# HGRN2's dots, level scores, values and states as 64 x 64 products in the quarters of TensorE

## Chip, core and metric

The kernel runs on one core of one Trainium2 chip. The metric is the device time of one execution in microseconds (us); of several runs the median is given. TensorE (PE) multiplies matrices, VectorE (DVE) and ScalarE (ACT) work element by element, GpSimd (POOL) and SyncE (SP) mostly start transfers here. SBUF is the working memory with 128 partitions; PSUM holds TensorE's results in eight banks of 128 x 512 float32.

## What is computed

A decoder trunk of two layers on 512 tokens of width 1024. Each layer is: half a SwiGLU feed-forward, a mixer with one input projection and one output projection over three groups of heads (short convolution, HGRN2, forgetting attention "FoX"), and again half a SwiGLU. Everything is float32. HGRN2 has 4 heads with 64 key and 64 value features and runs over 8 chunks of 64 tokens:

```python
bcum = jnp.cumsum(lfb, axis=-2)
rel = bcum[..., :, None, :] - bcum[..., None, :, :]
decay = jnp.where(causal, jnp.exp(jnp.where(causal, rel, 0.0)), 0.0)
scores = jnp.einsum('bhtd,bhsd,bhtsd->bhts', qb, kb, decay)
o = (jnp.einsum('bhts,bhsv->bhtv', scores, vb)
     + jnp.einsum('bhtd,bhdv->bhtv', qb * jnp.exp(bcum), state))
b_last = bcum[..., -1:, :]
state = (jnp.exp(b_last[..., 0, :])[..., None] * state
         + jnp.einsum('bhsd,bhsv->bhdv', kb * jnp.exp(b_last - bcum), vb))
```

After that o is normalised per head, scaled and gated.

## The kernel before

**The whole.** The feed-forwards take most of the time. Their weights and activations are split into a high and a low part for TensorE (`parted`, `granule`, the tiles `hl`), so each product is three matmuls (`mm3`, lines 308, 314, 315). The mixer's projections go the same way: `stream_steps` loads a granule of two k-tiles of weights by a transfer on SP's queue, ACT copies its high part (line 297), DVE subtracts to get the low part (line 298), and TensorE runs 24 matmuls on it. There are three buffers for split granules.

**HGRN2's stage** is the generator `hgrn` (line 1183), once for each pair of heads (`pr` 0 and 1), so four times in a run. The two heads of a pair lie in partitions 0 to 63 and 64 to 127 (features), and 512 tokens in the columns. `mix` (lines 1079 to 1087) steps the two generators by turns, and after each step it lets one granule of the FoX projections run (`dense`). That sets the program's order on every engine: a small burst of HGRN2's matmuls, then 24 matmuls of a projection, then the burst of the other pair. A scheduler may shift single instructions; each engine then runs its own queue in order.

The steps of one pair are:
- the decays, `b`, `k`, `kb` (to line 1209), and the transposed keys (line 1222);
- the chunks' own states U, 16 products of 64 rows by 64 columns (line 1244), each in one quarter of TensorE: its rows are chosen by the chunk's parity, its columns by the head, and the two row halves write to two PSUM banks. A scan on DVE joins them to the states S (line 1254), laid out as S[partition, v, chunk], with the chunk innermost;
- seven levels. The scores inside a chunk are split by the highest bit in which two tokens differ, so level `lev` joins the later half of each block of 2w tokens with its earlier half, w = 2^lev / 2. Levels 0 and 1 need only a dot product per token (`e` times `heads2`, line 1276; heads2 is a 128 x 2 matrix that sums each head's 64 features). Levels 2 to 6 make `e` (two DVE operations, lines 1302 and 1303, and an exponential on ACT), then `e2`, the later halves times the queries (line 1308), and multiply 128 tokens at a time, all 128 features held, against both heads' queries (line 1317). The two heads are kept apart by `q2`: a copy of q for each head in which the other head's 64 rows are zero (lines 1049 to 1055, with POOL's memsets and SP's copies). The scores of both chunks of a 128-token tile and of both heads come out, cross-chunk ones included; a predicated copy with a mask (line 1320) puts the wanted ones into A, a tile of [128, 2 heads, 4, 128];
- S2 (lines 1289 to 1295): the states copied by ACT into 128 x 128 blocks, one per chunk, zero off the two heads' diagonal blocks;
- the values (line 1331: 8 products, 128 x 64 held) and the states (line 1338: 7 products, S2's blocks held, 64 columns of `qe` moving) are summed in one PSUM bank of the tag "po";
- Square and a copy by ACT (lines 1344 and 1345), the mean by a matmul with `ones_blk` (line 1348), normalisation, gate and the split for the output projection (to line 1357).

PSUM banks go by tags: "mm" three, "sc" two, "pt" two, "po" one. All levels of both pairs take one "sc" bank each; U and the transposes take "pt"; the FoX projections take "mm" and once "po". The FoX projections' results are taken out of their banks by `fox_qkv` (lines 1395 to 1413), on ACT and DVE.

Of the kernel before, what the change touches and what calls it, by code (L numbers as in the profile page):

```python
# [8 lines left out]
F32 = mybir.dt.float32  # L9
F32R = mybir.dt.float32r  # L10
BF16 = mybir.dt.bfloat16
U8 = mybir.dt.uint8
# [11 lines left out]
P = 128  # L24
T = 512
# [19 lines left out]
CH = 64  # L45
# [111 lines left out]
class Trunk:  # L157
# [32 lines left out]
    def build_consts(self, scratch):  # L190
# [10 lines left out]
        self.heads2 = c.tile([P, 2], F32, tag="heads2", name="heads2")  # L201
        nc.vector.memset(self.heads2, 0.0)
        for h in range(2):
            nc.vector.memset(self.heads2[64 * h : 64 * h + 64, h : h + 1], 1.0)
# [8 lines left out]
        self.lmask = c.tile([P, 6, P], U8, tag="lmask", name="lmask")  # L213
# [16 lines left out]
        for l in range(1, 7):  # L230
            nc.vector.tensor_scalar(a, xf, scalar1=float(2 ** (l - 1)), scalar2=None, op0=ALU.is_ge)
            nc.vector.tensor_scalar(b, xf, scalar1=float(2**l), scalar2=None, op0=ALU.is_lt)
            nc.vector.tensor_mul(a, a, b)
            nc.vector.tensor_mul(self.lmask[:, l - 1, :], a, later)
# [733 lines left out]
    def mix(self, l, w, w_out, conv_w, out_gain, q_gain, k_gain, f_bias, next_gain):  # L968
# [3 lines left out]
        with tc.tile_pool(name=self.n("mix"), bufs=1) as mp:  # L972
# [47 lines left out]
            with tc.tile_pool(name=self.n("hg"), bufs=1) as hp:  # L1020
# [28 lines left out]
                q2 = [mp.tile([P, 2, T], F32, tag=f"hy{i}", name=self.n("q2")) for i in range(2)]  # L1049
                for i in range(2):  # L1050
                    nc.vector.tensor_mul(q[i], bq[i], inv)
                    for hh in range(2):
                        r = slice(64 * hh, 64 * hh + 64)
                        nc.gpsimd.memset(q2[i][r, 1 - hh, :], 0.0)
                        nc.sync.dma_start(q2[i][r, hh, :], q[i][r, :])
# [16 lines left out]
                run = [self.hgrn(l, pr, hp, z[pr], q[pr], q2[pr], v, sg[pr], og) for pr in range(2)]  # L1072
# [110 lines left out]
    def hgrn(self, l, pr, hp, z, q, q2, v, sg, og):  # L1183
# [76 lines left out]
        A = own("A", [P, 2, 4, P])  # L1260
        A8 = A.rearrange("p h i t -> p (h i) t")
        for lev in range(7):
# [3 lines left out]
            if lev < 2:  # L1266
# [7 lines left out]
                sb = self.bank("sc")  # L1274
                for i in range(4):
                    nc.tensor.matmul(
                        sb[:, i:8:4], e[:, i * P : (i + 1) * P], self.heads2, start=True, stop=True
                    )
                d = sb[:, :8].unsqueeze(2)
                if lev == 0:  # L1280
                    nc.vector.tensor_mul(
                        A8, self.ident.unsqueeze(1).to_broadcast([P, 8, P]), d.to_broadcast([P, 8, P])
                    )
                else:
                    m = self.lmask[:, 0, 1::2].unsqueeze(1).to_broadcast([P, 8, P // 2])
                    nc.vector.copy_predicated(A8[:, :, 1::2], m, d.to_broadcast([P, 8, P // 2]))


                    S2 = own("lk", [P, NCH - 1, P])
                    for hh in range(2):  # L1290
                        o = slice(64 * hh, 64 * hh + 64)
                        nc.gpsimd.memset(S2[o, :, 64 - 64 * hh : P - 64 * hh], 0.0)
                        nc.scalar.copy(
                            S2[o, :, o], S[o, :, : NCH - 1].rearrange("p v c -> p c v")
                        )
                yield
# [8 lines left out]


            e2 = tmp().rearrange("p (h t) -> p h t", h=2)
            nc.vector.tensor_mul(
                e2.rearrange("p h (n w) -> p h n w", w=w),
                half(e, 1).unsqueeze(1).to_broadcast([P, 2, n2, w]),  # L1310
                q2.rearrange("p h (n two w) -> p h n two w", two=2, w=w)[:, :, :, 1, :],
            )
            sb = self.bank("sc")
            s2 = sb.rearrange("p (h t) -> p h t", h=2)
            for i in range(4):
                t = slice(64 * i, 64 * i + 64)
# [303 lines left out]
```

## Time and profile before

| what | value |
|---|---|
| median of 3 runs | 1860.53 us (1856.95 to 1863.77) |
| the profiled execution | 1854.12 us |
| its span, first to last instruction | 1852.3 us |
| TensorE's granted clock | 1.000 |
| busy: POOL | 177.3 us (10%) |
| HGRN2's burst matmuls, PE busy over both layers | dots 7.6, levels 21.5, values 4.4, states 7.1 us |
| U's matmuls, PE busy over both layers | 2.8 us for 128 records |

A profile is of one execution. Its rows name the source line (L1317), the engine, the operation, output and input tiles with buffer numbers left out (`sc<-t,t`), the shape, how many, and how long. PE stands for matmuls and PEld for the loads of held operands; a float32 matmul shows as two records of each. Matmuls are pipelined and the end of each is modelled, so the times at which they start say more than their lengths. What ended an idle time is inferred from semaphores.

### The profile page before, as it was taken

To read this page: it belongs to the slowest core of one execution; us is meant where nothing else is said; L and a number is where in the kernel's file an instruction comes from. 1 tells how busy PE (TensorE), PEld (TensorE's weight loads), DVE (VectorE), ACT (ScalarE), POOL (GpSimd) and SP (SyncE) were. 2 spreads that over 40 slices of the span, in tenths; PEclk is the share of its full clock that TensorE was granted. 3 is DMA by queue.
4 is the path that set the end of the run, shared out by engine and by line. 5 is a ranking of instruction groups with operands and counts; after the bars stand their busy time and mean duration, and the time that the engine had idled before them with its cause. 6 is when DMAs were issued, how large, how long until landed. Compare 5 with 4: busy or idle time off the path is not lost.

```text
span 1852.3 us, 33371 instructions
## 1 busy us (share of the span) xinstructions
PE 1829.1 (99%) x13536; PEld 1700.0 (92%) x13536; DVE 1480.2 (80%) x2101; ACT 1007.3 (54%) x1467; POOL 177.3 (10%) x182
## 2 busy tenths in 40 slices
PE   8999999999999999999999999999999999999999
PEld 6899999899877899999889999998998788999997
DVE  7889787678787888878678887966868878888883
ACT  5455555564665555555445555545546664555552
POOL 0011120100000001112001111201000000020210
PEclk9999999999999999999999999999999999999999
DMA  7658783232223767868265787813323228577762
GB/s 205 171 121 190 182 176 96 69 95 73 75 75 97 209 131 170 186 170 171 81 200 127 163 192 185 171 59 90 81 64 87 80 91 228 148 160 194 150 136 91
DMA packets 245417, 251.90 MB, mean 136 GB/s; under 512 B 19568, under 2 KB 230000, under 8 KB 245264
## 3 DMA queue, kind: packets, MB, share of 16 engines
q1 hardware_dynamic: 191664, 183.69, 32.5%
q0 software_dynamic: 53600, 66.09, 22.3%
q8 instruction: 106, 1.74, 0.4%
q14 instruction: 47, 0.39, 0.1%
HBM read 223.98 MB, written 2.10 MB: 122 GB/s over the span
## 4 chain that ended last, share of the span: by engine, by line
PE 88%; DVE 6%; ACT 3%; issue 2%; DMA 1%; SPq 0%; ACTq 0%; DVEq 0%
PE mm L308 13%; PE mm L315 13%; PE mm L314 13%; PE sc L308 6%; PE sc L315 6%; PE sc L314 6%; PE pt L308 6%; PE pt L314 6%; PE pt L315 6%; PE po L308 3%; PE po L314 3%; PE po L315 3%; PE po L1472 1%; DVE hl L298 1%; PE pt L1513 1%
## 5 line engine op out<-in xcount | busy, mean ns | idle before, releaser
L766 ACT CAST hl<-w 128x1024 fp32r<-128x1024 f32 x322 | 337.2, 1049 | 317.2 <-PE mm L315 76.5
L768 DVE TENSOR_TENSOR hl<-w,hl 128x1024 fp32r<-128x1024 f32 x322 | 392.8, 1222 | 90.8 <-ACT hl L766 90.7
L298 DVE TENSOR_TENSOR hl<-st,hl 128x512 fp32r<-128x512 f32 (+2 forms) x196 | 166.5, 852 | 114.7 <-ACT hl L297 113.6
L297 ACT CAST hl<-st 128x512 fp32r<-128x512 f32 (+2 forms) x196 | 146.6, 750 | 184.8 <-PE mm L315 66.7
L308 PE MATMUL mm<-xc,hl 128*128 128x256 f32 (+1 forms) x732 | 201.7, 276 | 1.7 <-ACT g L872 1.4
L315 PE MATMUL mm<-xc,hl 128*128 128x256 f32 x728 | 201.4, 277 | 0.0
L314 PE MATMUL mm<-xc,hl 128*128 128x256 f32 x728 | 201.4, 277 | 0.0
L308 PE MATMUL sc<-xc,hl 128*128 128x256 f32 (+1 forms) x530 | 146.6, 277 | 2.4 <-ACT g L872 1.7
L315 PE MATMUL sc<-xc,hl 128*128 128x256 f32 x528 | 146.3, 277 | 0.0
L314 PE MATMUL sc<-xc,hl 128*128 128x256 f32 x528 | 146.2, 277 | 0.0
L308 PEld LDWEIGHTS mm<-xc,hl 128*128 128x128 f32 x732 | 137.4, 188 | 2.5 <-ACT g L872 1.8
L315 PEld LDWEIGHTS mm<-xc,hl 128*128 128x128 f32 x728 | 136.7, 188 | 0.1
L314 PEld LDWEIGHTS mm<-xc,hl 128*128 128x128 f32 x728 | 136.7, 188 | 0.0
L308 PE MATMUL pt<-xc,hl 128*128 128x256 f32 (+1 forms) x484 | 133.0, 276 | 0.0
L314 PE MATMUL pt<-xc,hl 128*128 128x256 f32 x480 | 133.0, 277 | 0.0
L315 PE MATMUL pt<-xc,hl 128*128 128x256 f32 x480 | 132.8, 277 | 0.0
L308 PE MATMUL mm<-hl,x 128*128 128x256 f32 (+1 forms) x384 | 112.3, 292 | 0.7 <-DVE qk L1403 0.3
L308 PE MATMUL mm<-x,hl 128*128 128x512 f32 x272 | 109.7, 403 | 0.0
L315 PE MATMUL mm<-hl,x 128*128 128x256 f32 (+1 forms) x384 | 107.4, 280 | 0.0
L314 PE MATMUL mm<-hl,x 128*128 128x256 f32 (+1 forms) x384 | 107.1, 279 | 0.0
L315 PE MATMUL mm<-x,hl 128*128 128x512 f32 x272 | 106.5, 392 | 0.0
L314 PE MATMUL mm<-x,hl 128*128 128x512 f32 x272 | 106.0, 390 | 0.0
(478 smaller groups left out, 5678.2 us busy)
## 6 DMA issues: line engine op xcount, KB each, us to landing
w<-in_ffn_w_in_dram SPq DMA_DIRECT2D x140, 512.0 KB, 5.5
w<-in_ffn_w_out_dram SPq DMA_DIRECT2D x64, 512.0 KB, 4.2
w<-in_ffn_w_out_dram POOLq DMA_DIRECT2D x56, 512.0 KB, 8.6
st<-in_w_mix_in_dram SPq DMA_DIRECT2D x88, 256.0 KB, 2.7
st<-in_ffn_w_in_dram SPq DMA_DIRECT2D x72, 256.0 KB, 3.1
w<-in_ffn_w_in_dram POOLq DMA_DIRECT2D x35, 512.0 KB, 8.5
w<-S POOLq DMA_DIRECT2D x35, 512.0 KB, 4.7
st<-in_ffn_w_out_dram SPq DMA_DIRECT2D x24, 512.0 KB, 3.6
```

Source lines behind the costliest of these rows:

```text
L297: a = nc.scalar.copy(hi, src[:, c : c + w])
L298: b = nc.vector.tensor_sub(lo, src[:, c : c + w], hi)
L308: i = nc.tensor.matmul(acc[:, c], ah, bh[:, c], start=first and c.start == 0, stop=False, skip_group_check=True,)
L314: nc.tensor.matmul(acc, ah, bl, start=False, stop=False, skip_group_check=True)
L315: i = nc.tensor.matmul(acc, al, bh, start=False, stop=last, skip_group_check=True)
L766: A(nc.scalar.copy(hi, src))
L768: return lambda: V(nc.vector.tensor_sub(lo, src, hi))
L1472: nc.tensor.matmul(self.ob[:, t0 + u * P : t0 + 2 * P], V[:, j, h % 4].rearrange("p a d -> p (a d)"), part[:, j, u:, :].rearrange("p i t - ...
L1513: nc.tensor.transpose(tb[:, j * P : (j + 1) * P], p[:, j * P : (j + 1) * P], self.ident)
```

## The change

It does the following, for each pair of heads:
- `q2` goes, with its memsets on POOL and its copies on SP; `e2` is `e`'s later half times q, 256 columns instead of 512.
- A new inner function `scores` makes each level from 16 products: 64 features of one head held for one chunk, against that head's and chunk's queries (32 columns), or against a column of ones (1 column) for the dots. The row half is the head, the column half the chunk's parity, and the two heads write to two banks.
- A is [128, 2, 4, 64]: the parity of the chunk lies in the partition halves, so masks are 64 wide (`lmask`, `ident2`) and a level's predicated copy is two, one per head, of a quarter of the elements each.
- Pair 0 takes both "sc" banks and pair 1 both "pt" banks for a level and for the output; the mean takes "po".
- S2 goes, with its memsets and ACT's copies: S itself is the held operand of the states, 14 products of 64 x 64 in the two quarters on the diagonal.
- The states come before the values, with a step between them, and the values are 16 products in all quarters. The output lies in two banks: ACT copies from them, DVE adds the part that the other bank holds, and Square reads the sum from SBUF.

Changed line numbers: the changed file is five lines longer at its end. The core of the diff (constants left out):

```diff
-    def hgrn(self, l, pr, hp, z, q, q2, v, sg, og):
+    def hgrn(self, l, pr, hp, z, q, v, sg, og):
...
-        A = own("A", [P, 2, 4, P])
-        A8 = A.rearrange("p h i t -> p (h i) t")
+        A = own("A", [P, 2, 4, CH])
+        rows = [slice(CH * x, CH * x + CH) for x in range(2)]
+        tag = ("sc", "pt")[pr]
+
+        def scores(held, moving, n):
+            sb = [self.bank(tag) for _ in range(2)]
+            for i in range(4):
+                for hh, par in ((0, 0), (1, 1), (0, 1), (1, 0)):
+                    c = 2 * i + par
+                    nc.tensor.matmul(
+                        sb[hh][rows[par], i * n : (i + 1) * n],
+                        held[rows[hh], c * CH : (c + 1) * CH], moving(rows[hh], c),
+                        start=True, stop=True,
+                    )
+            return [x[:, : 4 * n] for x in sb]
...
-                    S2 = own("lk", [P, NCH - 1, P])
-                    for hh in range(2):
-                        o = slice(64 * hh, 64 * hh + 64)
-                        nc.gpsimd.memset(S2[o, :, 64 - 64 * hh : P - 64 * hh], 0.0)
-                        nc.scalar.copy(
-                            S2[o, :, o], S[o, :, : NCH - 1].rearrange("p v c -> p c v")
+                for hh, d in enumerate(scores(e, lambda r, c: self.ones_c[r, :], 1)):
+                    n = CH >> lev
+                    d = d.unsqueeze(2).to_broadcast([P, 4, n])
+                    if lev == 0:
+                        nc.vector.tensor_mul(
+                            A[:, hh], self.ident2.unsqueeze(1).to_broadcast([P, 4, n]), d
                         )
+                    else:
+                        m = self.lmask[:, 0, 1::2].unsqueeze(1).to_broadcast([P, 4, n])
+                        nc.vector.copy_predicated(A[:, hh, :, 1::2], m, d)
...
+            e2 = tmp()[:, : T // 2]
             nc.vector.tensor_mul(
...
+                e2.rearrange("p (n w) -> p n w", w=w), half(e, 1), half(q, 1)
+            )
+            sb = scores(e, lambda r, c: e2[r, 32 * c : 32 * c + 32], 32)
+            for hh in range(2):
+                nc.vector.copy_predicated(
...
+        ob = [self.bank(tag) for _ in range(2)]
+        for c in range(1, NCH):
+            for hh in range(2):
                 nc.tensor.matmul(
...
+                    ob[hh][rows[hh], c * CH : (c + 1) * CH], S[rows[hh], :, c - 1],
+                    qe[rows[hh], c * CH : (c + 1) * CH],
+                    start=c == 1, stop=False, skip_group_check=True,
                 )
...
+        yield
         for i in range(4):
...
+            for par, hh in ((0, 0), (1, 1), (0, 1), (1, 0)):
+                c = 2 * i + par
                 nc.tensor.matmul(
...
+                    ob[par][rows[hh], c * CH : (c + 1) * CH],
+                    v[rows[par], i, pr * P + 64 * hh : pr * P + 64 * hh + 64],
+                    A[rows[par], hh, i, :], start=i == 0 and par != hh, stop=i == 3,
+                    skip_group_check=True,
                 )
...
-        nc.scalar.activation(sq, ob, AF.Square)
-        nc.scalar.copy(o, ob)
+        every = lambda a, c: a.rearrange("p (c t) -> p c t", t=CH)[:, c::2, :]
+        for hh in range(2):
+            f, mine, other = rows[hh], ob[hh], ob[1 - hh]
+            nc.scalar.copy(o[f, hh * CH :], mine[f, hh * CH :])
+            if hh:
+                nc.scalar.copy(o[f, :CH], other[f, :CH])
+            c = 1 + hh
+            nc.vector.tensor_add(every(o[f, :], c), every(o[f, :], c), every(other[f, :], c))
+        nc.scalar.activation(sq, o, AF.Square)
         yield
-        mb = self.bank("sc")
+        mb = self.bank("po")
```

71 lines of the change are left out of this document (19 added, 52 removed).

## The prediction

> **What bounds the kernel now.** I read the page first, then busy time by stage, then TensorE's (PE's) instructions in order of time.
>
> ```profile
> PE 1829.1 (99%) x13536; PEld 1700.0 (92%) x13536; DVE 1480.2 (80%) x2101; ACT 1007.3 (54%) x1467; POOL 177.3 (10%) x182
> PE 88%; DVE 6%; ACT 3%; issue 2%; DMA 1%; SPq 0%; ACTq 0%; DVEq 0%
> ```
>
> The second line is the chain that ended last: PE holds 88% of it. A busy PE need not be at its peak, but there is hardly an idle one to fill: a change pays only through PE time that it takes out, or through waits of PE. The HGRN2 stage stands in each layer at about 390 to 478 us and 1300 to 1392 us. The worst stretch of it in each layer (columns: window, us, busy time of PE, PEld, DVE, ACT, POOL, clock, DMA share, GB/s):
>
> ```profile
> 416.00:430.00 14.00, 12.96 (x109) 12.44 (x108) 13.54 (x31) 6.46 (x15) 0.00 (x0) 1.00 0.29 77
> 1330.00:1343.00 13.00, 11.97 (x99) 11.46 (x98) 12.58 (x29) 5.89 (x15) 0.00 (x0) 1.00 0.25 73
> ```
>
> Here VectorE (DVE) is full and PE idles a microsecond. PE's own rows show where (start, length, group; in brackets the idle time ahead and what ended it):
>
> ```profile
> 420.62 1.13 PE L1317 MATMUL sc<-t,t 128*128 128x128 f32 x8 [0.29 <-DVE fm L1398]
> 425.69 1.13 PE L1317 MATMUL sc<-t,t 128*128 128x128 f32 x8 [0.39 <-DVE t L1308]
> 429.53 0.68 PE L1317 MATMUL sc<-t,t 128*128 128x128 f32 x4 [0.36 <-DVE t L1308]
> 454.94 0.36 PE L308 MATMUL mm<-hl,x 128*128 128x256 f32 x1 [0.17 <-DVE ft L395]
> 474.10 0.36 PE L308 MATMUL mm<-hl,x 128*128 128x256 f32 x1 [0.17 <-DVE qk L1403]
> ...
> 1334.00 1.13 PE L1317 MATMUL sc<-t,t 128*128 128x128 f32 x8 [0.29 <-DVE fm L1398]
> 1339.07 1.13 PE L1317 MATMUL sc<-t,t 128*128 128x128 f32 x8 [0.29 <-DVE t L1308]
> 1342.92 1.13 PE L1317 MATMUL sc<-t,t 128*128 128x128 f32 x8 [0.44 <-DVE t L1308]
> ```
>
> Six waits are at the first score bursts of the levels. Everywhere else in the stage the projection's matmuls run without a gap, and HGRN2's small bursts are let in between groups of 24 of them.
>
> **The change, term by term: the bursts.** What a burst costs PE is read from the starts of its neighbours.
>
> ```profile
> 397.35 0.28 PE L314 MATMUL mm<-hl,x 128*128 128x256 f32 x1
> 397.46 0.28 PE L315 MATMUL mm<-hl,x 128*128 128x256 f32 x1
> 397.67 0.69 PE L1244 MATMUL pt<-v,t 64*64 64x64 f32 x32
> 398.29 0.38 PE L308 MATMUL mm<-hl,x 128*128 128x256 f32 x1
> 398.51 0.29 PE L314 MATMUL mm<-hl,x 128*128 128x256 f32 x1
> ...
> 404.58 0.28 PE L315 MATMUL mm<-hl,x 128*128 128x256 f32 x1
> 404.70 0.95 PE L1276 MATMUL sc<-heads,t 128*128 128x2 f32 x8
> 405.50 0.36 PE L308 MATMUL mm<-hl,x 128*128 128x256 f32 x1
> 405.70 0.28 PE L314 MATMUL mm<-hl,x 128*128 128x256 f32 x1
> ...
> 435.89 0.28 PE L315 MATMUL mm<-hl,x 128*128 128x256 f32 x1
> 436.01 1.05 PE L1317 MATMUL sc<-t,t 128*128 128x128 f32 x8
> 436.82 0.36 PE L308 MATMUL mm<-hl,x 128*128 128x256 f32 x1
> 437.02 0.28 PE L314 MATMUL mm<-hl,x 128*128 128x256 f32 x1
> ...
> 458.33 0.28 PE L315 MATMUL mm<-hl,x 128*128 128x256 f32 x1
> 458.53 1.09 PE L1331 MATMUL po<-A,v 128*64 128x128 f32 x16
> 459.56 1.77 PE L1338 MATMUL po<-qe,lk 128*128 128x64 f32 x14
> 461.14 0.36 PE L308 MATMUL mm<-hl,x 128*128 128x256 f32 x1
> 461.34 0.28 PE L314 MATMUL mm<-hl,x 128*128 128x256 f32 x1
> ```
>
> Projection matmuls start every 0.11 us (397.35 to 397.46). From the start of the last one ahead of a burst to that of the second one behind it, less two such steps (0.23), is the burst's cost: dots (L1276) 405.70 - 404.58 - 0.23 = 0.89 us; scores of a level (L1317) 1.13 - 0.23 = 0.90; values and states (L1331, L1338) 3.01 - 0.23 = 2.78. An f32 matmul shows as two records, so x8 is four matmuls.
>
> The first group, L1244, is the form that the change gives to everything: 16 products of 64 rows by 64 columns by 64, over the four quarters in turn. It costs 398.51 - 397.46 - 0.23 = **0.82 us**, entry and exit included: 32 records in 0.62 us (19.4 ns each) and 0.20 around them. The new bursts move 1 or 32 columns instead of 64. That this hardly matters I take from the dots, which move 2 columns where the levels move 128 and differ by 0.01: 0.81. From below, a burst that shrank with its columns would be half of 0.62 and 0.20, 0.51; from above, quarters that run two at a time give 1.44 (a rival).
>
> Per pair of heads: two dots and five levels, 2 x 0.89 + 5 x 0.90 = 6.28, become 7 x 0.81 = 5.67: 0.61 saved, with two pairs in two layers 4 x 0.61 = **2.4 us**.
>
> Values become one burst of 16 such products, 0.82. States become 14 products, by turns in two of the quarters: 14 turns. Their held operand is now S itself, read with 8 elements (32 bytes) from one column to the next, as L1293 reads it today:
>
> ```profile
> L1293 ACT COPY lk<-S 64x448 f32<-64x448 f32 x8 | 8.8, 1094 | 0.1
> L1345 ACT COPY t<-po 128x512 f32<-128x512 f32 x4 | 2.3, 580 | 0.0
> L1281 DVE TENSOR_TENSOR A<-ident,sc 128x1024 f32<-128x1024 f32 x4 | 4.9, 1216 | 1.1 <-PE sc L1276 1.1
> L1286 DVE COPY_PREDICATED A<-lmask,sc 128x512 f32<-128x512 uint8 x4 | 5.3, 1332 | 0.6 <-PE sc L1276 0.5
> L1320 DVE COPY_PREDICATED A<-lmask,sc 128x512 f32<-128x512 uint8 x20 | 16.8, 839 | 0.1
> L1308 DVE TENSOR_TENSOR t<-t,q 128x512 f32<-128x512 f32 x20 | 13.8, 688 | 3.8 <-ACT t L262 3.5
> L1302 DVE TENSOR_TENSOR t<-kb,b 128x256 f32<-128x256 f32 x20 | 8.3, 417 | 0.0
> L396 DVE TENSOR_SCALAR ft<-ft 128x8 f32<-128x8 f32 x16 | 2.6, 164 | 0.1
> ```
>
> ScalarE (ACT) takes 1094/448 = 2.44 ns an element there and 580/512 = 1.13 in a plain copy: 2.16 times as long. No row shows PE with a strided held operand. If the stride costs nothing, 14 turns at L1244's pace (0.62/8 = 0.078) and 0.20 are 1.29 us. If it costs what ACT pays: L1338 spends 1.58/14 = 0.113 on a load of 128 columns, half of that on 64, 2.16 times that is 0.122, so 14 x 0.122 + 0.20 = 1.91. I take 1.91, the row of the same tensor and stride. Then 2.78 - 0.82 - 1.91 = 0.05, times 4 = **0.2 us**; with 1.29, 2.7.
>
> The Trainium skill, "Advanced Engine Details and Errata", section "SBUF Cachelines", speaks against this edit: lines are 16 bytes and need two hits each for full speed, so S at 32 bytes is read at a penalty, for which it gives no figure. L1293 agrees (2.16 times); by that page the term is the 0.2, and without it the 2.7.
>
> **DVE, ACT and the waits.** A short operation's floor is L396's 0.164 us. By it, a quarter of the elements costs: L1281 0.43, L1286 0.46, L1320 0.33; half of L1308 is L1302's 0.417. Over both layers: L1281 4.9 to 8 x 0.43 = 3.4, L1286 5.3 to 3.7, L1320 16.8 to 40 x 0.33 = 13.3, L1308 13.8 to 8.3, together 12 us less on DVE ahead of the values; behind them 8 additions of 64x256 are new, 3.3 at most. ACT loses L1293's 8.8, which today stand ahead of the first levels' exponentials, and gains some 0.7 per pair of heads (a copy of 512 columns on one half is replaced by copies of 512, 448 and 64).
>
> Up to 430 us a layer's DVE loses 2 x 0.36 (L1281), 2 x 0.42 (L1286), 2 x 0.17 (two L1320) and 3 x 0.27 (L1308), 2.7 us, against 1.04 of idle PE in brackets. In the changed program's order the e2 product of the first level stands right behind level 1's copies, and two groups of 24 matmuls and a burst (6.3 us) lie between those copies' burst and its own. So I take the six waits as gone. Each is its bracket plus 0.28 - 0.11 = 0.16 by which matmuls otherwise overlap: 2.07 + 6 x 0.16 = **3.0 us**. From below none goes (0).
>
> What is late next: the waits at 454.94 and 474.10, for the fox projections' PSUM banks. They stay: DVE reaches those products (L1403) after the last levels' copies and the new additions, by my count within 0.3 us of today.
>
> Added waits: ACT's copies of o wait for the values burst, DVE's additions for the copies, Square for the additions, the mean's matmul for Square. Behind the copies in ACT's queue stands one granule's split, which PE wants after both means. The chain (three copies, two additions, Square) is some 2.7 us, with the fox work between under 5; PE has 48 projection matmuls and a burst, 6.3 us, before the first mean. Cost nothing; if that cover went, up to 2 us a layer.
>
> At nothing: both halves' bank waits ride on a burst's first two matmuls, as in L1244; SP's 8 copies of q and POOL's 16 memsets go, for which PE waits nowhere; a few constants more on DVE at the start, about 0.6 us beside matmuls.
>
> **Sum:** 2.4 + 0.2 + 3.0 = 5.6 us. The profiled execution, 1854.1 (span 1852.3 and 1.8 around it), becomes 1848.5. It lies 6.4 below the median of the runs, 1860.5; against that I forecast **1854.9**.
>
> **Rivals.** *The stride is free to PE:* 2.4 + 2.7 + 3.0 = 8.1, **1852.4**. For it: PE is another reader than ACT. Against: L1293.
> *PE's waits stay:* another DVE product takes the place of L1308. 2.6, **1857.9**. Against: 2.7 us less DVE work ahead of 1.04 idle.
> *Narrow quarters don't run four at a time* (place: the 28 dots and level bursts and 4 values bursts): at two at a time 2 x 0.62 + 0.20 = 1.44 each, 32 x 0.63 = 20 us lost, 14.5 slower, **1875.0**. It decides from 19.4 + 5600/(32 x 32) = 25 ns a record on. Against: L1244's 19.4.
> The skill's "TensorE: Matmul & The Clock Gate", section "Wait — 56ns, not 53.3ns?", has starts never closer than about 25 ns however few columns. By that rule a burst is 32 x 25 + 200 ns = 1.00, the sum 0.5 slower, 1861.0. The trace disagrees with 0.62 us for 32 records.
> That the change doesn't do what it says is excluded: the changed order shows the quarter products in place of the padded ones.
>
> **Chances.** Forecast 0.45, free stride 0.27, waits stay 0.15, two at a time 0.08, the 25 ns floor 0.05. A measurement tells about 0.3% (5.6 us) from no change: half of the forecast's case and nearly all of the free stride's lie beyond it: faster 0.47; the rest of both, the waits and the floor 0.37; slower 0.16, two at a time and unforeseen bank waits. The range goes from 1849.5 (free stride, and a third of the way to bursts of 0.51: 28 x 0.10 = 2.8 more) to 1862.5 (waits stay, with the runs' own spread of 3 us).
>
> **What would show it.** In the changed profile: level and dot bursts at 0.81 between neighbours; the states' burst at 1.9 (stride) or 1.3; no L1317-like bracket in 416 to 430; DVE some 9 us lower, ACT 5 or more. I am wrong if a burst is over 1.0, if new brackets stand ahead of the level bursts, or if PE waits on fox banks for longer than 0.2.

## The result and the profile after

The changed kernel takes **1856.88 us** (median of 21 runs, 1851.17 to 1864.29) beside 1861.6 for the kernel before (21 runs, 1854.07 to 1866.07). The ratio is 0.9979 with a 95% interval of 0.9969 to 0.9989. By the ratio that is 3.9 us faster (2.0 to 5.8), by the medians 4.7; the forecast was 5.6 (1854.9 for the time). That is 0.2%, less than the 0.3% that the prediction took as the least a measurement can tell; with 21 runs of each the interval still excludes no change. The profiled execution has a span of 1850.5 us, 1.8 below before's.

Two lines of the page after, in answer to those of before:

```profile
PE 1827.9 (99%) x14328; PEld 1693.2 (92%) x14328; DVE 1469.2 (79%) x2143; ACT 1004.1 (54%) x1467; POOL 168.7 (9%) x166
PE 88%; DVE 6%; ACT 3%; issue 1%; DMA 1%; SPq 1%; ACTq 0%
```

PE still carries the chain. DVE lost 11.0 us, ACT 3.2 (the prediction had 5 or more), POOL 8.6. The two worst windows of before, after the change (same columns):

```profile
416.00:430.00 14.00, 14.00 (x226) 13.36 (x225) 13.22 (x43) 7.53 (x17) 0.00 (x0) 1.00 0.28 78
1330.00:1343.00 13.00, 13.00 (x191) 12.50 (x190) 12.63 (x41) 6.84 (x17) 0.00 (x0) 1.00 0.27 71
```

PE idled 1.04 and 1.03 us there, now not at all; DVE is still nearly full. The new bursts between their neighbours on PE (a dot step, a level, the states, in order of time):

```profile
406.14 0.28 PE L319 MATMUL mm<-hl,x 128*128 128x256 f32 x1
406.35 0.64 PE L1268 MATMUL sc<-ones_c,t 64*64 64x1 f32 x32
406.92 0.39 PE L312 MATMUL mm<-hl,x 128*128 128x256 f32 x1
407.14 0.28 PE L318 MATMUL mm<-hl,x 128*128 128x256 f32 x1
...
437.83 0.28 PE L319 MATMUL mm<-hl,x 128*128 128x256 f32 x1
438.04 0.67 PE L1268 MATMUL pt<-t,t 64*64 64x32 f32 x32
438.64 0.38 PE L312 MATMUL mm<-hl,x 128*128 128x256 f32 x1
438.86 0.29 PE L318 MATMUL mm<-hl,x 128*128 128x256 f32 x1
...
455.53 0.28 PE L319 MATMUL mm<-hl,x 128*128 128x256 f32 x1
455.74 1.90 PE L1325 MATMUL sc<-qe,S 64*64 64x64 f32 x28
457.57 0.39 PE L312 MATMUL mm<-hl,x 128*128 128x256 f32 x1
457.79 0.28 PE L318 MATMUL mm<-hl,x 128*128 128x256 f32 x1
```

By the prediction's way of reading (start of the second one behind, less start of the last one ahead, less 0.23): a dot step 407.14 - 406.14 - 0.23 = **0.77**, a level 438.86 - 437.83 - 0.23 = **0.80**, the states 457.79 - 455.53 - 0.23 = **2.03**. A values burst is 0.82, as forecast (466.11 - 465.06 - 0.23).

In the stage, PE now waits here:

```profile
469.92 0.36 PE L312 MATMUL mm<-hl,x 128*128 128x256 f32 x1 [1.09 <-DVE ft L399]
483.87 0.47 PE L312 MATMUL mm<-x,hl 128*128 128x512 f32 x1 [0.20 <-DVE V L1415]
...
1382.09 0.36 PE L312 MATMUL mm<-hl,x 128*128 128x256 f32 x1 [1.09 <-DVE ft L399]
```

The six brackets ahead of level bursts and the four of 0.17 at fox banks are gone. In each layer a bracket of 1.09 is new, and a smaller one later (0.20, in the second layer 0.11). The large one stands at a bank of the fox projections. The engine is named rightly, the line not quite, as its neighbours on ACT and DVE show (the same timeline, other engines):

```profile
466.58 0.57 ACT L1345 COPY t<-sc 64x512 f32<-64x512 f32 x1
...
467.40 0.21 ACT L266 ACTIVATE fr<-fr 128x8 f32<-128x8 f32 x1
467.64 0.21 ACT L266 ACTIVATE ft<-fr 128x8 f32<-128x8 f32 x1
467.88 0.53 ACT L1345 COPY t<-sc 64x448 f32<-64x448 f32 x1
...
467.32 0.40 DVE L1349 TENSOR_TENSOR t<-t,sc 64x256 f32<-64x256 f32 x1
...
468.49 0.17 DVE L1407 TENSOR_TENSOR fr<-fr,invc 128x8 f32<-128x8 f32 x1
468.69 0.36 DVE L1349 TENSOR_TENSOR t<-t,sc 64x192 f32<-64x192 f32 x1
469.08 0.69 DVE L1408 TENSOR_TENSOR qk<-mm,fr 128x512 f32<-128x512 f32 x1
```

The product at line 1408 reads the fox bank; it ends at 469.77, and PE starts 0.15 later. Its scale `fr` was ready at 468.66, but the output's second addition (line 1349) stood ahead: 0.42 us. And ACT's part of `fr` stood behind the output's copies, from 466.58 to 467.40: 0.8 us. Together that is 1.2, enough for the 1.09.

**Where the time went.** To compare profiles I count PE's projection matmuls, which are the same ones in every kernel here (12324 in each), and read the start of the k-th. The HGRN2 stage of the first layer lies between the 2700th and the 3600th, that of the second between the 8950th and the 9800th. This takes out what differs elsewhere between single executions. A second profile of the kernel before agrees with the first to 0.25 us in the first layer's stretch and 0.1 in the second's.

| kernel | stage 1, us beside before | stage 2 | both |
|---|---|---|---|
| changed | -2.5 | -2.5 | **-5.0** |
| contiguous states | -4.2 | -4.1 | -8.2 |
| one more step before o | -0.2 | -1.3 | -1.5 |
| step moved | -4.5 | -4.3 | -8.9 |
| quarter by quarter | +8.1 | +8.4 | +16.5 |
| both winning edits | -6.2 | -6.2 | -12.5 |
| both, with narrow masks | -5.7 | -5.9 | -11.5 |
| wide e2; dead copies; e2 and a free product; all load in place | -2.4 to -2.5 | -2.4 to -2.5 | -4.9 to -5.0 |

At the start of the program the changed kernel loses some of it: its 300th projection matmul starts at 84.95 us instead of 83.33. Experiment 6 splits that.

### The profile page after: what moved, and what is told of

Read it like the earlier page. It is cut to its first block, busy times and chain, and to the rows that moved or that the text cites. A ratio compares the mean times of both kernels' runs of the same rounds, so it can differ in the third digit from the quotient of the medians.

```text
span 1850.5 us, 34941 instructions
## 1 busy us (share of the span) xinstructions
PE 1827.9 (99%) x14328; PEld 1693.2 (92%) x14328; DVE 1469.2 (79%) x2143; ACT 1004.1 (54%) x1467; POOL 168.7 (9%) x166
## 4 chain that ended last, share of the span: by engine, by line
PE 88%; DVE 6%; ACT 3%; issue 1%; DMA 1%; SPq 1%; ACTq 0%
PE mm L312 13%; PE mm L319 13%; PE mm L318 13%; PE sc L312 6%; PE sc L319 6%; PE sc L318 6%; PE pt L318 6%; PE pt L312 6%; PE pt L319 6%; PE po L312 3%; PE po L318 3%; PE po L319 3%; DVE hl L302 1%; PE po L1477 1%; PE pt L1518 1%
```

## The experiments

**1. The states from contiguous columns.** The theory: the states' burst is long because the held operand is read with a stride of 32 bytes. The rival: two quarters by turns are slow in themselves.

```diff
                         nc.vector.copy_predicated(A[:, hh, :, 1::2], m, d)
+                if lev:
+                    Sc = own("lk", [P, NCH - 1, HD])
+                    nc.scalar.copy(Sc, S[:, :, : NCH - 1].rearrange("p v c -> p c v"))
...
-                    ob[hh][rows[hh], c * CH : (c + 1) * CH], S[rows[hh], :, c - 1],
+                    ob[hh][rows[hh], c * CH : (c + 1) * CH], Sc[rows[hh], c - 1, :],
```

> The changed kernel, with the states copied once per pair by ACT at level 1 into a tile with the columns side by side (448 elements on 128 partitions, as the old lk copy but in one instruction), and that tile held in the states' products. Stride theory (the 32 byte stride makes the weight load slow): the states' burst falls from 2.03 us between its neighbours to about 1.3 (14 turns at U's pace of 0.078 plus 0.20), 4 x 0.74 = 3.0 us less in all, loads of the held operand at 135 ns as in the other quarter products instead of 214; ACT gains 4 x 1.1 = 4.4 us, hidden if the first levels have slack now. Time near 1854. Rival (the two diagonal quarters by turns are slow in themselves): the burst stays at 2.0, loads stay above 200 ns, time 1857 or a little more.

Measured: 1853.14 us (10 runs), before 1859.98 on the same chip, ratio 0.9961 (0.9942 to 0.9981). The states' burst in its profile, and then the weight loads of both kernels (min, median and max of one, in ns):

```profile
455.66 0.28 PE L319 MATMUL mm<-hl,x 128*128 128x256 f32 x1
455.87 1.03 PE L1328 MATMUL sc<-qe,lk 64*64 64x64 f32 x28
456.83 0.38 PE L312 MATMUL mm<-hl,x 128*128 128x256 f32 x1
457.05 0.28 PE L318 MATMUL mm<-hl,x 128*128 128x256 f32 x1
```

```profile
L1325 PEld LDWEIGHTS sc<-qe,S x56: 192/214/215, 455.7 to 1369.4; 64*64 64x64 f32 x56
```

```profile
L1328 PEld LDWEIGHTS sc<-qe,lk x56: 129/135/135, 455.9 to 1366.8; 64*64 64x64 f32 x56
```

457.05 - 455.66 - 0.23 = 1.16 us instead of 2.03, the load 135 ns instead of 214: the stride was the cost, 0.87 us a pair and 3.5 in all, of which the stages show 3.3. (By the runs alone this kernel is not clear of the changed one: the intervals of the two ratios overlap.) ACT's copy of 1.08 us per pair brought no wait. The same 28 records need 0.96 us instead of 1.83.

**2. One more step ahead of the output's copies.** The theory for the new wait of 1.09: the output's copies and additions stand in the queues ahead of the fox product that frees the bank.

```diff
                     skip_group_check=True,
                 )
+        yield
         o, sq, r, t = tmp(), tmp(), tmp(), tmp()
```

> The changed kernel with one more step between the values and the copies of the output, so that one more granule of the FoX projections stands ahead of the copies, the additions and Square in every queue. Theory (the new 1.09 us wait of PE in each layer, at 468.8 and 1381.0, is there because DVE's fox product that frees the bank stands behind the output's additions, which wait for ACT's copies): that bracket falls below 0.3 in both layers, about 1.0 to 1.3 us a layer less on PE, 2 to 2.5 in all, time near 1854.5. Rival (the bank is late because of the fox chain itself, Square to product): the bracket stays at about 1 us. Second rival: the wait moves to the end of the stage, where the mean and the normalisation are one granule later: a bracket of 1 us or more ahead of the output projection or of the last means, time 1857 to 1860.

Measured: 1858.29 us (10 runs), before 1859.98, ratio 0.9998 (0.9983 to 1.0013): the gain is gone. The bracket fell only to 0.83. The compiled order explains it: the second addition (its line is 1350 here) still runs right ahead of the fox product, at 469.22 and 469.61. The edit did not separate them, so it says nothing against the theory, but my expectation of it was wrong. The second rival came true in part: between 483 and 530 us the first layer's brackets of PE grew from 0.7 us in the changed kernel to 2.3, at a mean (0.34), the convolution (0.53) and the attention (0.66), none of them the 1 us that it had named.

**3. The step moved behind the values.** Same number of steps; states and values in one stretch, as in the kernel before.

```diff
                     start=c == 1, stop=False, skip_group_check=True,
                 )
-        yield
         for i in range(4):
...
                     skip_group_check=True,
                 )
+        yield
         o, sq, r, t = tmp(), tmp(), tmp(), tmp()
```

> The changed kernel with the step that stands between states and values moved behind the values: states and values in one stretch, then a granule, then copies, additions and Square. The number of steps is that of the changed kernel. Theory as for the kernel with one more step: the 1.09 us bracket goes, 2 to 2.5 us less, time near 1854.5, and nothing is later at the end of the stage than in the changed kernel. Rival: the bracket stays near 1 us, time 1857.

Measured: 1849.26 us (4 runs), before 1859.98, ratio 0.9944 (0.9924 to 0.9964). The bracket is gone in both layers (a later one is 0.30 instead of 0.20 and 0.11), DVE's additions now run at 464.59 and 465.59, ahead of the fox chain, and the stages are 3.9 us shorter together than the changed kernel's, more than the 2.5 I expected. The rest is in the burst itself:

```profile
456.11 0.28 PE L319 MATMUL mm<-hl,x 128*128 128x256 f32 x1
456.31 1.78 PE L1325 MATMUL sc<-qe,S 64*64 64x64 f32 x26
457.81 0.33 PE L1333 MATMUL sc<-A,v 64*64 64x64 f32 x3
457.92 0.29 PE L1325 MATMUL sc<-qe,S 64*64 64x64 f32 x2
457.93 0.75 PE L1333 MATMUL sc<-A,v 64*64 64x64 f32 x29
458.61 0.39 PE L312 MATMUL mm<-hl,x 128*128 128x256 f32 x1
458.83 0.28 PE L318 MATMUL mm<-hl,x 128*128 128x256 f32 x1
```

458.83 - 456.11 - 0.23 = 2.49 us where states and values apart cost 2.03 + 0.82 = 2.85. One entry and exit of a burst is saved, and the first values start before the last states: 0.36 a pair, 1.4 in all. The step that the change put between states and values cost that, and the wait.

**4. Quarter by quarter.** The prediction's dearest rival was that narrow quarters don't run side by side. Here the order of issue alone is changed.

```diff
-            for i in range(4):
-                for hh, par in ((0, 0), (1, 1), (0, 1), (1, 0)):
+            for hh, par in ((0, 0), (1, 1), (0, 1), (1, 0)):
+                for i in range(4):
                     c = 2 * i + par
```

> The changed kernel with the 16 products of each dot and level burst issued quarter by quarter (four in the same quarter after each other) instead of by turns over the four quarters. If products in different quarters run beside each other only when they follow each other in the queue: 32 records one at a time, at 0.078 a turn 2.5 us and 0.2 around them, 2.7 instead of 0.79 per burst, 28 bursts x 1.9 = 53 us slower, 1910. If the load of one hides behind the product before whatever the quarter: near 0.8, no change, 1857. Two at a time (the price of the prediction's rival): 1.44, 18 us slower, 1875.

One execution: 1878.05 us, the stages 21.5 us longer than the changed kernel's. A level's burst:

```profile
437.27 0.28 PE L319 MATMUL mm<-hl,x 128*128 128x256 f32 x1
437.47 1.43 PE L1268 MATMUL pt<-t,t 64*64 64x32 f32 x32
438.83 0.38 PE L312 MATMUL mm<-hl,x 128*128 128x256 f32 x1
439.05 0.29 PE L318 MATMUL mm<-hl,x 128*128 128x256 f32 x1
```

439.05 - 437.27 - 0.23 = 1.55 us against 0.80, 28 x 0.75 = 21. It is near the rival's price (1.44), not the 2.7 of one at a time: even within one quarter a product overlaps the one before it, for its 32 records start within 1.36 us, 42 ns each, while a load takes 135. So these bursts pay only because neighbours in the queue lie in different quarters.

**5. What the six waits hung on.** Three kernels put back parts of the load, a fourth all of it: the product e2 over 512 columns; ACT's copies of the states; e2 and a further DVE product per dot step; and e2, the doubled first operation on A and ACT's copies together. The edits:

```diff
-            e2 = tmp()[:, : T // 2]
+            e2 = tmp()
             nc.vector.tensor_mul(
-                e2.rearrange("p (n w) -> p n w", w=w), half(e, 1), half(q, 1)
+                e2.rearrange("p (h n w) -> p h n w", h=2, w=w),
+                half(e, 1).unsqueeze(1).to_broadcast([P, 2, n2, w]),
+                half(q, 1).unsqueeze(1).to_broadcast([P, 2, n2, w]),
             )
```

> The changed kernel with the product e2 made over 512 columns again (the second half is a repeat that nobody reads): DVE does 20 x 0.27 = 5.4 us more, nothing else changes. In the changed profile the first level's burst at 416.87 starts 0.64 us after its e2 ended, the next 1.23, the following 2.9, where in the kernel before each waited (0.15 after). If DVE's load at the levels was what the six waits hung on by itself: brackets of 0.1 to 0.4 come back at the first bursts, some 1 us slower than the changed kernel. If it takes more than e2: the first burst starts some 0.35 us after its e2, no bracket, the stage within 0.3 us of the changed kernel's.

One execution: 1854.51 us; no bracket at a level burst, stages as in the changed kernel.

```diff
+                if lev:
+                    Sc = own("lk", [P, NCH - 1, HD])
+                    for x in range(2):
+                        nc.scalar.copy(
+                            Sc[rows[x]], S[rows[x], :, : NCH - 1].rearrange("p v c -> p c v")
+                        )
```

> The changed kernel with ACT's two copies of the states per pair put back at level 1, as before, into a tile that nobody reads: ACT does 8 x 1.09 = 8.8 us more, DVE and PE the same. If the six waits hung on ACT's copies, which stood ahead of the first levels' exponentials: brackets come back at the first two or three level bursts, 1 to 3 us slower than the changed kernel. If they hung on DVE's load: no bracket at the level bursts, the stage within 0.3 us of the changed kernel's.

One execution: 1850.56 us; no bracket. ACT has 8 copies more of 1.06 us each.

```diff
+                dd = own("dd", [P, T // 2])
+                nc.vector.tensor_mul(dd, q[:, : T // 2], q[:, : T // 2])
                 yield
                 continue
```

> The changed kernel with DVE's load ahead of the levels put back as it was: e2 over 512 columns (20 x 0.27) and, in each dot step, one more product of 256 columns into a tile that nobody reads (8 x 0.41, in place of the wider operations on A); 8.7 us of DVE in all, ACT and PE as changed. The wide e2 alone left the first bursts 0.37, 0.96 and 0.36 us after their e2. If the six waits hung on DVE's load: brackets come back at one or more of the first three bursts, 0.3 to 1 us slower a layer. If they hung on the order of DVE's queue or on the single bank of scores and not on its load: no bracket at the level bursts, stage within 0.3 us of the changed kernel's.

One execution: 1854.94 us; no bracket. The free product was scheduled at 388 us, ahead of the stage, so this run tested no more than the wide e2.

```diff
-                    if lev == 0:
-                        nc.vector.tensor_mul(
-                            A[:, hh], self.ident2.unsqueeze(1).to_broadcast([P, 4, n]), d
-                        )
-                    else:
-                        m = self.lmask[:, 0, 1::2].unsqueeze(1).to_broadcast([P, 4, n])
-                        nc.vector.copy_predicated(A[:, hh, :, 1::2], m, d)
+                    for _ in range(2 - hh):
+                        if lev == 0:
+                            nc.vector.tensor_mul(
+                                A[:, hh], self.ident2.unsqueeze(1).to_broadcast([P, 4, n]), d
+                            )
+                        else:
+                            m = self.lmask[:, 0, 1::2].unsqueeze(1).to_broadcast([P, 4, n])
+                            nc.vector.copy_predicated(A[:, hh, :, 1::2], m, d)
```

(and with it the wide e2 and ACT's two copies, as above)

> The changed kernel with all of the load that the change took away ahead of the levels put back where it stood: e2 over 512 columns (DVE, 20 x 0.27), the first of each dot step's two operations on A done twice (DVE, 8 x 0.43, after the dots, so that it can't be moved ahead), ACT's two copies of the states per pair at level 1 (8 x 1.09). The former try with a free product put its 8 x 0.41 at 388 us, ahead of the stage, so it did not test this. In the compiled order the first level's e is now made behind level 1's copies of pair 0, as in the kernel before; in the changed kernel it is made ahead of them. If load, with the order that follows from it, is what the six waits hung on: brackets of 0.2 to 1 us at one to three of the first level bursts in each layer, stage 0.5 to 2 us a layer longer than the changed kernel's. If it was something else (the one bank per burst, the order of the pairs' bursts): no bracket at the level bursts, stage within 0.3 us a layer of the changed kernel's.

One execution: 1859.82 us beside 1857.19 of before, with stages as short as the changed kernel's (the time outside them holds two of the slow stretches told of at the end): still no bracket. But the margin is nearly gone. The first level's e2 and its burst in the changed kernel, then with the load in place:

```profile
415.77 0.46 DVE L1307 TENSOR_TENSOR t<-t,q 128x256 f32<-128x256 f32 x1
...
420.37 0.67 PE L1268 MATMUL sc<-t,t 64*64 64x32 f32 x32
```

```profile
420.93 0.72 DVE L1314 TENSOR_TENSOR t<-t,q 128x512 f32<-128x512 f32 x1
...
422.33 0.67 PE L1268 MATMUL sc<-t,t 64*64 64x32 f32 x32
```

From the end of e2 (start and length) to the burst: 4.14 us in the changed kernel, 0.68 with the load in place. (The 0.64 and 0.37 in two of the expectations set each e2 beside the burst ahead of its own; by the right pairing the first three margins are 4.15, 4.76 and 6.47 in the changed kernel, 3.88, 4.49 and 3.90 with the wide e2, 4.17, 4.76 and 6.46 with the dead copies, 0.68, 0.36 and 0.34 with all of it.) In the kernel before a burst that waited started 0.15 us after its e2. So all the load together eats 3.5 to 6 us of margin, with e made behind level 1's copies again; neither the wide e2 nor ACT's copies alone do (the doubled operation was not tried alone); and the last 0.2 to 0.5 us up to a wait, and the waits of 0.29 to 0.44 themselves, are not accounted for. DVE is still 3.2 us less busy than in the kernel before (1477.0 against 1480.2). The levels' predicated copies were longer before (the first one at 422.00 took 1.31 us, now there are two of 0.45), and that was not put back; whether it is the rest, is not settled. The other rival, that in the kernel before all levels shared two banks, was not tried by itself.

**6. The start of the program.** The changed kernel builds more constants on DVE. First the kernel before with as many operations:

```diff
         nc.vector.tensor_copy(self.identb, self.ident)
+        for par in range(2):
+            r = slice(CH * par, CH * par + CH)
+            nc.vector.tensor_copy(self.identb[r, :], self.ident[r, :])
...
-            nc.vector.tensor_mul(self.lmask[:, l - 1, :], a, later)
+            for par in range(2):
+                r = slice(CH * par, CH * par + CH)
+                nc.vector.tensor_mul(self.lmask[r, l - 1, :], a[r, :], later[r, :])
```

> The kernel before with as many constants built on DVE at the start as in the changed kernel (12 mask products of 64 rows instead of 6 of 128, and 2 copies more; their results are those of before). In four profiles of the changed forms PE's 300th projection matmul, at 83 us, stands 1.6 to 2.4 us later than in the one profile of before, and the wait for DVE at about 60 us is 1.74 instead of 1.06. If the constants are the cause: the same 1.74 and some 1.6 us later here. If it is the spread of single executions or something else in the change: 1.06 and a start within 0.5 of before's.

One execution: 1864.93 us, the 300th matmul 7.8 us late: neither figure. It lost far more than the change. Its wait at 61 us was 3.53, and then PE ran at half its clock (a window of the same profile: column eight is the granted clock):

```profile
65.06 0.76 PE L313 MATMUL sc<-x,hl 128*128 128x512 f32 x1 [3.53 <-DVE gi L535]
```

```profile
60.00:65.00 5.00, 1.53 (x7) 0.94 (x5) 5.00 (x6) 2.14 (x3) 0.00 (x0) 0.93 0.34 107
65.00:70.00 5.00, 4.94 (x12) 3.91 (x13) 5.00 (x9) 1.21 (x2) 0.00 (x0) 0.50 0.31 105
```

> The kernel before once more, unchanged, for a second profile of its opening. If the constants put the changed kernel's opening back: PE's 300th projection matmul within 0.4 us of 83.3 and a wait for DVE near 60 us of about 1.06. If it was the spread of single executions: anywhere up to 85.5. The six waits at the level bursts as in the first profile, 0.28 to 0.45 each.

One execution: 1859.34 us, the 300th matmul 1.07 late, the wait 1.06, the six waits as in the first profile (0.29 to 0.44).

Last, the masks built from 64 columns, in the kernel with both winning edits:

```diff
-        a = scratch(F32)[:, :P]
-        b = scratch(F32)[:, :P]
+        a, b = scratch(F32), scratch(F32)
+        a, b, x2, later2 = a[:, :CH], b[:, :CH], a[:, CH:P], b[:, CH:P]
+        for par in range(2):
+            r = slice(CH * par, CH * par + CH)
+            nc.vector.tensor_copy(x2[r, :], xf[r, r])
+            nc.vector.tensor_copy(later2[r, :], later[r, r])
...
-            for par in range(2):
-                r = slice(CH * par, CH * par + CH)
-                nc.vector.tensor_mul(self.lmask[r, l - 1, :], a[r, r], later[r, r])
+            nc.vector.tensor_mul(self.lmask[:, l - 1, :], a, later2)
```

> The kernel with both winning edits (contiguous held states, step moved behind the values), and the level masks built at the start from 64 columns instead of 128: six times four operations of 64 columns, and four copies ahead of them, instead of six times three of 128 columns and two of 64 x 64; about 2.5 us less DVE work at the start. If DVE's constants are what puts the start of the changed forms back by 1.4 to 2.4 us: PE's 300th projection matmul at or below the 83.3 us of before, the wait for DVE at 60 us near 1.06 or less, and 1.5 to 2 us less than the kernel with the two edits, so a ratio near 0.9917 and 1844.5. If the opening's time is spread or has another cause: that matmul at 85 us, no difference from 0.9927.

The same wait in before, the changed kernel and this one:

```profile
60.10 0.47 PE L308 MATMUL sc<-x,hl 128*128 128x512 f32 x1 [1.06 <-DVE gi L530]
```

```profile
61.69 0.47 PE L312 MATMUL sc<-x,hl 128*128 128x512 f32 x1 [1.74 <-DVE gi L534]
```

```profile
60.40 0.47 PE L314 MATMUL sc<-x,hl 128*128 128x512 f32 x1 [0.32 <-DVE gi L536]
```

It is 1.06 in both profiles of before, 1.71 to 1.74 in the ten of the changed forms, 0.32 here, and the 300th matmul comes at 83.6 us. But the length of this wait says only where three of PE's matmuls stand: 131 projection matmuls run ahead of the wait before it (at 45 to 47 us) in the kernel before, 134 in the changed forms, 128 here, and 192 ahead of this one in all. What puts the start back comes earlier. The mask products stand in DVE's queue behind a split of weights and ahead of the small products of the tile `lb`; ACT waits for `lb`, and behind that, in ACT's queue, stands its part of a norm on which the following work depends (before, the changed kernel, narrow masks):

```profile
40.60 0.21 ACT L262 ACTIVATE lb<-lb 128x4 f32<-128x4 f32 x1 [3.05 <-DVE lb L962]
```

```profile
42.20 0.20 ACT L266 ACTIVATE lb<-lb 128x4 f32<-128x4 f32 x1 [3.85 <-DVE lb L966]
```

```profile
40.92 0.21 ACT L268 ACTIVATE lb<-lb 128x4 f32<-128x4 f32 x1 [2.65 <-DVE lb L968]
```

From the start of that split to ACT's `lb` it is 3.01 us in both profiles of before, 3.81 to 3.83 in the ten of the changed forms and 2.61 with narrow masks; from there to the end of the wait at 60 us it is 19.5 in all of them. So the constants cost the changed kernel **0.8 us**; the other 0.8 of its late start is there when the split starts, and two executions of the kernel before differ by more (1.05). In the kernel before with more constants the stretch is 5.12, because they are 128 columns wide there and more of them stand ahead of `lb`. Its 7.8 us are 1.7 at the split, these 2.1, 1.1 for another split that runs ahead of the product `gi` in DVE's queue, and 2.9 at half the clock. In time the narrow masks can't be told: 1848.67 us (6 runs), before 1856.91 on that chip, ratio 0.9948 (0.9928 to 0.9968), against 0.9927 without them. Their stages are 0.9 us longer, for a wait of 0.95 and 0.71 ahead of the attention that was 0.34 and 0.32.

**7. Both winning edits together** (experiments 1 and 3).

> Both edits that won by themselves: the states copied side by side before they are held, and the step between states and values moved behind the values. If the two are independent, their stage gains add: against the changed kernel's profile each layer's HGRN stage shortened by 1.6 with the first and by 1.9 with the second, so 3.5 a layer, 7.0 in all, against before about 12 less in the stage, and 1.5 to 2 given back at the start of the program: time 1849 to 1851 beside a before of 1860. The states' burst 1.2 to 1.3 us, no wait of PE at the fox projections' banks. If they overlap (the contiguous burst only moves PE into a wait): no better than the second alone, whose ratio was 0.9944.

Measured: **1845.97 us** (6 runs), before 1860.17, ratio **0.9927 (0.9907 to 0.9947)**. The stages are 12.5 us shorter than before's, 7.5 shorter than the changed kernel's, where the parts alone gave 3.3 and 3.9: they add up. The time is below the 1849 to 1851 expected. It beats both kernels.

## Why the prediction held, and where it did not

| step | forecast | measured, both layers |
|---|---|---|
| bursts of dots and levels | 2.4 | 4 x (2 x 0.12 + 5 x 0.10) = 3.0 |
| values and states | 0.2 | 4 x (2.78 - 2.85) = -0.3 |
| six waits | 3.0 | 3.0, all gone |
| waits at fox banks | 0 | -1.8 |
| constants | 0 | -0.8 |
| sum | 5.6 | 3.1; ratio 3.9, stages alone 5.0 |

The waits are reckoned as in the forecast, bracket plus 0.16: at the fox banks 4 x 0.33 went and 2 x 1.25, 0.36 and 0.27 came. The stages' 5.0 is 1.1 more than their four terms (3.9). Of this, 0.5 is the six waits, which this way of reckoning makes too small: read from their neighbours, the bursts that waited cost 1.43 to 1.57 us in the kernel before (the first one 421.71 - 420.05 - 0.23), 0.58 more than the 0.90 of the others in the mean, 3.5 for the six. The other 0.6 I can't put to a cause.

*Bursts.* Right: a dot step at 0.77 and a level at 0.80 against 0.81; that they hardly shrink with their columns held (0.77 for 1, 0.80 for 32, 0.82 for 64). Four at a time held because of the order (experiment 4). The gain is small because of what stands around the records: in the traces, records of one quarter start 58 ns after one another, so the eight rounds of a burst take 0.46 us where eight records of 128 x 128, 112 ns apart, take 0.90; but some 0.3 of entry and exit come on top. The Trainium skill, "TensorE: Matmul & The Clock Gate", section "Wait — 56ns, not 53.3ns?", has starts never closer than about 25 ns; the trace disagrees: 32 records between 438.04 and 438.64, 19 ns each. Within one quarter the starts are never that close (58 ns).

*States.* Right in mechanism, and a little small in size: 2.03 against 1.91, on the ratio that ACT paid for the same tensor. Experiment 1 shows that it is the stride. That the size came so near is luck in part: the contiguous turn is 0.069 us, not the 0.057 that went into it, and the stride makes it 1.9 times as long, not 2.16; the two errors offset each other. The Trainium skill, "Advanced Engine Details and Errata", section "SBUF Cachelines", said that there would be a penalty; the trace agrees, with 214 ns a load against 135.

*The six waits.* The outcome was right. The reason was too simple: I set 2.7 us less DVE work against 1.04 us of idle PE. Experiment 5 shows that the margin is 4 to 6 us, that neither the wide e2 nor ACT's copies take it away by themselves, and that with all the load back, and the first level's e behind level 1's copies as before, 3.5 to 6 us of it go. I had seen that order, but not weighed it. The waits themselves did not come back, so what made the last half microsecond of them stays open.

*The fox banks.* This step failed: "DVE reaches those products (L1403) after the last levels' copies and the new additions, by my count within 0.3 us of today." The old waits of 0.17 went, and a new one of 1.09 in each layer came. I had named what stands behind the output's copies in ACT's queue as "one granule's split", and missed the fox normalisation, whose exponentials stand there too (467.40 and 467.64); and I had counted the new additions as a load, not as instructions that wait while the fox product stands behind them. The prediction had named a wait on fox banks of more than 0.2 as a sign of being wrong, and it came. Experiment 3 shows that the place of the step decides it. How much of the 1.09 is the copies and how much the additions was read from the queue (0.8 and 0.42), and not tried apart.

*Constants.* "Beside matmuls" was no cover: the masks stand in DVE's queue ahead of `lb`, for which ACT waits, and PE waits at 60 us for what follows from it. 0.8 us.

*A cost that I had not seen as one:* the step between states and values. It costs 0.36 us a pair besides the wait.

Of the rivals, the free stride is refuted by experiment 1, the two at a time by the profile; its price came true in experiment 4. PE's waits did go. The forecast was 1 to 2 us too good: two losses that I had at nothing (1.8 and 0.8) and values and states (0.5) stand against bursts that gave 0.6 more, waits that gave 0.5 more and the 0.6 without a cause. The 5.6 still lies in the interval of the runs (2.0 to 5.8), but in part because these errors offset each other. The upper end of the range, 1862.5, does not come out of its own terms (1857.9 and 3 make 1860.9); the measured 1856.88 lies inside either.

## What to carry to other kernels

A small product in a quarter of TensorE pays when its neighbours in the queue lie in the other quarters and its held operand is contiguous; check both before counting instructions. When a chain of copies and additions is put ahead of an existing chain on the same two engines, write out what else stands behind each waiting instruction, bank releases above all, and try the chain one step earlier or later: the place of one step was worth as much here as the whole change. Constants at the start of a program are free only where nothing that PE will wait for, even by way of another engine, stands behind them in the queue.

## What the runs showed of the hardware

- A held operand of 64 columns at 32 bytes from one to the next: 214 ns a load and 0.131 us a turn (1.83 us for 14), contiguous 135 ns and 0.069 (0.96 for 14).
- In the traces' single records, those of one quarter start 58 ns after one another whether 1, 32 or 64 columns move (120 ns with the strided operand), and those of the four quarters 6 to 7 ns apart; records of 128 x 128 start 112 ns apart, with 2 columns as with 128 (lines 1276 and 1317 of the kernel before).
- Experiment 6: after PE had idled 3.53 us, its matmuls of 512 columns started every 0.43 us instead of 0.23 for 6 us (65.06 to 71.1), at a granted clock of 0.50. Waits of 1.74 us did not do that. The Trainium skill, "TensorE: Matmul & The Clock Gate", section "Part 1: The HAM clock gate (the "warmup" mystery)", has the clock halved after an idle window of about 3.4 us; this run agrees. But 3.76 us of idle time that ended at 9.48 us in the same run were not followed by it (granted clock 1.00 from 9 to 12 us), so these runs fix no threshold.
- In eight of the fourteen profiles a feed-forward has a stretch of some 110 us in which each projection matmul takes 3.9% longer at an unchanged granted clock: 172 matmuls in 20 us instead of 179, here in the kernel with both edits and in the changed one. It costs about 4 us, as much as this whole change, and is why single executions were compared by the stages; its cause is open.

```profile
740.00:760.00 20.00, 20.00 (x172) 20.00 (x171) 17.02 (x18) 11.59 (x14) 4.75 (x4) 1.00 0.94 173
```

```profile
740.00:760.00 20.00, 20.00 (x179) 20.00 (x178) 17.78 (x19) 11.39 (x13) 5.80 (x5) 1.00 0.86 160
```
